# A two-layer streaming encoder step on one core: norms summed and spread by one wide product, norm weights loaded with x, sample softmax transposed a step later, and prompt scores as three float32r products

## The chip, the cores and the metric

The kernel runs on one core of one Trainium2 chip. The metric is the device time in microseconds of one execution; the time before is the median of three runs. The profile is of one further execution. PE is TensorE (matmuls), PEld its weight loads, DVE is VectorE, ACT is ScalarE, POOL is GpSimd, SP is SyncE, which issues most DMAs. The kernel writes matmuls of two kinds: float32, which the trace shows as two records each, and float32r, which it shows as one.

## The reference

An encoder of two layers reads a prompt of 256 frames and a sample of 32 frames with a cache of 128. The width is 1024, heads have 64 features.

```
layer 0: x += concat(8 chunked softmax heads with a relative bias,
                     8 stick-breaking heads) @ w_out_ab
layer 1: x += 16 forgetting heads @ w_out_c      # softmax(q k / 8 + cum_q - cum_k)
both:    x += 4-head cross-attention(rmsnorm(x)) into 256 memory rows
         x += (silu(h @ w_gate) * (h @ w_up)) @ w_down,  h = rmsnorm(x)
rmsnorm(x) = x * rsqrt(mean(x * x) + 1e-6) * g       # 7 norms of x, 1 of the memory's rows a layer
```

Outputs are the final norm of both streams and the new keys, values, log-forget values and memory keys and values. Everything is float32.

## The kernel before

Activations are held with features on partitions: `x` is eight tiles of 128 features by 288 tokens (256 prompt tokens and 32 of the sample). Every weight matrix comes in units of 128 x 1024 (512 KB). `unit` loads one by a DMA of SP into `st`, ACT casts it to float32r (`hi`, L156), and DVE subtracts (`lo`, L157). The normed input is split likewise into `hh` and `hl`, and `mm3` (L183) makes each block of a projection from three float32r products (hh hi, hl hi, hh lo), so that about float32 precision results. A unit of eight blocks is 24 products of 288 columns into one accumulator `pj`, of which there are four. The down projection of the feed-forward part is `dn`, the output projections are `op`, the memory's values `mv`.

The norm is split off: `Next.block` multiplies x by the norm's weight `gain` only and projects that; the token's scale `rstd` is applied when an accumulator is evacuated (L668, L760, L762, L795, L802). `Norm.add` squares each block on ACT (`sq`) and adds it up on POOL, the last on DVE (`ssq`). `columns` (L266) sums over the partitions by three float32 products against `mean1`, of two columns each (`nrm`), and `newton` (L275) makes the inverse root by eleven DVE operations on 128 x 6 numbers; `rows` (L287) spreads it over all partitions by three more products (`nr`), and ACT copies the result into `rstd` (L331). Until then, evacuations are held back in `waiting`. `begin` starts two units with six of eight blocks before the last blocks of x are there, and calls `columns` behind the first unit.

Attention is written as generators, which `tick` advances by one step after each unit, so that attention work stands between projections. `attend_prompt` (L414) handles a pair of heads, which lie in the two halves of the partitions: it transposes v (`vt`), multiplies q and k of each head in float32 (`sc`, 64 rows, 128 and 256 columns), and runs `softmax` (L394) on DVE and ACT into `e`; two steps later it transposes the weights (`tp`) and one step after that multiplies by v (`po`). `attend_sample` (L451) does the same for four heads of the sample (`ss`, `es`, `ts`, `os`, then `ot`). In layer 1 the bias `bc` of a pair is made on POOL (L1001 to L1004) from a row `ck`, which comes by a DMA. The gate's own product is `gp`, and its logits are folded by `gt` after rstd.

The order on each engine is set by the scheduler of the framework when the program is built; each engine then runs its own instructions strictly in that order. `not_before` adds an order by hand.

Of the kernel before, what the change touches and what calls it, by code (L numbers as in the profile page):

```python
# [15 lines left out]
P = 128  # L16
# [10 lines left out]
def encoder_step(ctx: ExitStack, tc: tile.TileContext, a):  # L27
# [21 lines left out]
    def tok(s, dt=F32):  # L49
        return tk.tile([P, NT], dt, tag="t", name=name(s))  # L50
# [19 lines left out]

    gain = cst.tile([P, 9 * KT], F32, name="gain")
    xh = [big.tile([P, 2 * NT], F32, tag=f"x{i}", name=f"x{i}") for i in range(4)]
    x = [xh[k // 2][:, (k % 2) * NT:(k % 2) * NT + NT] for k in range(KT)]

# [5 lines left out]

    def x_part(i, eng=DMA):
        eng.dma_start(xh[i], a["xT"][:, 2 * i * NT:2 * (i + 1) * NT])

    first_part(0, 0, 384)
    x_part(0)
    x_part(1, S)
    x_part(3, S)
    DMA.dma_start(gain, a["gains"])
    first_part(0, 384, 1024)
    first_part(1, 0, 1024)  # L90
    x_part(2)
    first_part(2, 0, 1024)


    mean1 = cst.tile([P, 2], F32, name="mean1")
    G.memset(mean1, 1.0 / 1024.0)
    identb = cst.tile([P, P], BF16, name="identb")
    make_identity(nc, identb)


    line = cst.tile([8, 384], F32, name="line")
    lined = dr.tile([8, 384], F32, name="lined")
# [37 lines left out]
    def more_constants():  # L140
        V.tensor_scalar(ident, warm[:, 0:P], 1.0 / 32.0, None, op0=ALU.mult)
        by_head = ident.rearrange("p (j i q) -> p j i q", j=2, i=2)
        V.tensor_tensor(fold, by_head[:, :, 0], by_head[:, :, 1], ALU.add)
        V.tensor_tensor(fold4, fold[:, 0, 0:16], fold[:, 1, 0:16], ALU.add)
        V.tensor_copy(ntrir, ntri)

# [52 lines left out]
    def begin(srcs, cur):  # L199


        out = []
        for src in srcs:
            w, p = unit(src), acc("pj")
            for k in range(BEGIN):
                mm3(p[:, :NT], w, k, cur.h, k, k == 0, False)
            out.append((w, p))
            if len(out) == 1:
                cur.y = cur.norm.columns()
        return out  # L210
# [30 lines left out]
    class Norm:  # L241
# [7 lines left out]
        def add(self, xb, eng=None):  # L249
            q = tok("sq")  # L250
            S.activation(q[:, :self.n], xb[:, :self.n], AF.Square)  # L251
            self.parts += 1
            eng = eng or (V if self.parts == KT else G)
            i = int(self.parts == KT and self.hurry)
            if self.acc[i] is None:
                self.acc[i] = q
            else:
                s = tok("ssq")
                eng.tensor_tensor(s[:, :self.n], self.acc[i][:, :self.n], q[:, :self.n], ALU.add)  # L259
                self.acc[i] = s  # L260

        def sum(self, p, part, begin):
            for i, t in enumerate(self.tiles):
                mm(p[:, 2 * i:2 * i + 2], part[:, t:t + 128], mean1, begin and i == 0, False)

        def columns(self, between=None):  # L266
            p = att("nrm")
            self.sum(p, self.acc[0], True)
            if between:
                between()  # L270
            if self.acc[1] is not None:
                self.sum(p, self.acc[1], False)
            return self.newton(p)

        def newton(self, p):  # L275
            c = len(self.tiles)
            v, y, t = small("ms"), small("y"), small("nt")
            v, y, t = v[:, :2 * c], y[:, :2 * c], t[:, :2 * c]
            V.tensor_scalar(v, p[:, :2 * c], EPS, None, op0=ALU.add)
            V.tensor_scalar(y.bitcast(I32), v.bitcast(I32), -0.5, 1597463007.0, op0=ALU.mult, op1=ALU.add)  # L280
            for _ in range(3):
                V.tensor_tensor(t, y, y, ALU.mult)
                V.scalar_tensor_tensor(t, t, -0.5, v, op0=ALU.mult, op1=ALU.mult)
                self.last = V.scalar_tensor_tensor(y, t, 1.5, y, op0=ALU.add, op1=ALU.mult)
            return y

        def rows(self, y):  # L287

            p = att("nr")
            for i, t in enumerate(self.tiles):  # L290
                a0 = 256 if i == 2 else t
                mm(p[:, a0:t + 128], y[:, 2 * i:2 * i + 1].to_broadcast([P, P]), ident[:, a0 - t:P], i == 0, True)
            return p[:, :self.n]

# [10 lines left out]
    class Next:  # L305


        def __init__(self, gi):
            self.gi, self.norm, self.h, self.waiting = gi, Norm(hurry=gi == 8), ([], []), []
            self.y = None  # L310

# [12 lines left out]

        def scale(self):

            if self.gi == 0:
                yield 1
            p = self.norm.rows(self.y)
            self.r = big.tile([P, NT], F32, tag="rstd", bufs=2, name=name("rstd"))  # L330
            r = S.copy(self.r, p)  # L331
            done = [f() for f in self.waiting]
            self.waiting = None
            if self.gi == 0:
                behind.append(self.norm.last.ins)
                yield 1
                behind.extend([r.ins, done[-1].ins])

# [75 lines left out]
    def attend_prompt(q, k, v, vns, j, bias, oh, ol, at=None, falling=False):  # L414

        q0, q1 = (q[:, 160:288], q[:, 32:160]) if falling else (q[:, 0:128], q[:, 128:256])
        vn = vns[j] = v_natural(v)
        e = []
        for hd in range(2):
            r = slice(64 * hd, 64 * hd + 64)  # L420
            s = att("sc")
            mm(s[:, 0:128], q0[r], k[r, 0:128])
            mm(s[:, 128:384], q1[r], k[r, 0:256])
            e.append(work("e"))
            softmax(s, QT, bias[hd], e[hd], at)
# [25 lines left out]
    def attend_sample(qs, ks, two, vns, ck, cv, bias, o, falling=False):  # L451
# [7 lines left out]
        e = work("es")  # L459
        softmax(s, [(0, 160)], bias, e)  # L460
        yield 1
        t = att("ts")
# [115 lines left out]
    def mem_scales():  # L578
        y = memn.columns()
        V.tensor_copy(memcol, y.rearrange("p (t two) -> p t two", two=2)[:, :, 0])  # L580
        S.copy(memrow, memn.rows(y))

    class Memory:
# [28 lines left out]
        def step(self):  # L612
# [10 lines left out]
            else:  # L623
# [15 lines left out]
                if half == 1:  # L639
                    for t in range(2):  # L640
                        v = tok("mv")
                        V.tensor_scalar(v[:, 0:NP], self.p[:, 256 * t:256 * t + 256], memcol[:, t:t + 1], None, op0=ALU.mult)
                        store(a["mv"][l, t, :, hd * 256:hd * 256 + 256], v[:, 0:NP])
                        self.v[t, hd] = split(v[:, 0:NP], tok("vh", F32R)[:, 0:NP], tok("vl", F32R)[:, 0:NP])


    def cross(layer, cur, memory, nxt):
        o = ([tok("oh", F32R) for _ in range(KT)], [tok("ol", F32R) for _ in range(KT)])
        q, qs = [], []
        begun = begin([a["w_xq"][layer, f] for f in range(2)], cur)  # L650
        active.append(cur.scale())

# [101 lines left out]
    def ffn(layer, cur, nxt, ahead):  # L754
        h = ([], [])
        active.append(cur.scale())

# [64 lines left out]
    def mix_ab(cur, nxt, memory, w0):  # L822
# [6 lines left out]
        def side_by_side():  # L829
            p = [att("pj"), acc("pj"), acc("pj")]  # L830
            with tc.issue_after(warmed.ins):
                for k in range(KT):
                    for u in range(3):
                        b = 3 * k + u
                        i = mm3(p[u][:, :NT], w0[b // 8], b % 8, cur.h, k, k == 0, k == KT - 1)
                        if k in (0, 5, 7) and u == 2:
                            began.append(i.ins)
            cur.y = cur.norm.columns()
            tick()
            return p  # L840

        def proj(j):
# [7 lines left out]
            if j < 4:  # L850
                biases[j] = [rel_prompt(2 * j + i) for i in range(2)]
            vs[j] = evac_kv(cur, next(p), a["kv0"][kv + 4])

# [20 lines left out]

        active.append(cur.scale())
        pairs(proj, attend, sample, memory, (0, 0, 0, 0, 2, 2, 2, 8))
# [99 lines left out]
    def mix_c(cur, nxt, memory, w0):  # L976
# [3 lines left out]
        begun = begin([w[0], w[8]], cur)  # L980
        active.append(cur.scale())
        p = att("gp")
# [55 lines left out]
    cur.norm.add(x[KT - 1], V)  # L1038
    more_constants()
    memories = [Memory(0), Memory(1)]  # L1040
# [46 lines left out]
def _pack(inputs):  # L1087
# [17 lines left out]
    def vals(c):  # L1105
# [3 lines left out]
    gains = np.stack([g["g_mix"][0], g["g_mix"][1], g["g_xattn"][0], g["g_xattn"][1], g["g_mem"][0], g["g_mem"][1],  # L1109
                      g["g_ffn"][0], g["g_ffn"][1], g["g_final"]])  # L1110
    w_ab = units(g["w_in_ab"][0])
# [3 lines left out]
    out = {  # L1115
        "xT": feats(x), "memT": feats(g["mem_prompt"][0]),
        "gains": gains.reshape(9, 8, 128).transpose(2, 0, 1).reshape(128, 72),
        "w_ab": w_ab, "w_first": w_ab[[0, 4, 8]].reshape(3, 128, 8, 128).transpose(1, 2, 0, 3).reshape(128, 3, 1024).transpose(1, 0, 2), "w_oab": units(g["w_out_ab"][0]),
# [41 lines left out]
```

## Time and profile before

| | |
|---|---|
| median of 3 runs | 957.79 us (957.63 to 958.33) |
| profiled execution | 958.14 us, span 956.4 us |
| first projection product, first norm's sum | 7.26 us, 18.88 us |
| softmax heads of layer 0, of layer 1 | up to about 75 us, 515 to 635 us |
| cross-attention | about 191 to 247 us and 657 to 713 us |
| feed-forward | 270 to 480 us and 737 to 945 us |
| last norm and output | from 945.5 us |

A row of a group shows line, engine, operation, what it writes and reads, shape and count, then the busy time in us and the mean ns of one, then the engine's idle time ahead of it and what ended it. A row of the timeline starts with the start and the length in us. A row of the chain of waits has start, length, and what was waited for or done. Matmuls overlap: the length of one record is longer than its distance to the next, and the distance is what counts.

### The profile page before, as it was taken

What the parts mean: (1) busy time and instruction counts of PE and PEld (TensorE: products, weight loads), DVE (VectorE), ACT (ScalarE), POOL (GpSimd) and SP (SyncE); (2) the same over time, 40 slices, a digit from 0 to 9 for tenths busy, and PEclk for the clock granted to TensorE, in tenths of its full rate; (3) what the DMA queues carried; (4) which work ended last, traced back from release to release, by engine and by line L of the source; (5) the groups of instructions that cost most, each with busy time, mean ns of one, the idle gap of its engine ahead of it and who ended that gap; (6) DMA issues with size and microseconds to landing.
All of it is one profiled execution on the core that took longest, in us unless ns stands there. A gap on an engine that the chain in (4) does not pass through costs nothing.

```text
span 956.4 us, 19036 instructions
## 1 busy us (share of the span) xinstructions
PE 943.6 (99%) x7476; PEld 915.0 (96%) x7476; DVE 587.3 (61%) x1137; ACT 483.8 (51%) x860; POOL 237.2 (25%) x358
## 2 busy tenths in 40 slices
PE   8999999999999999999999999999999999999997
PEld 8988999999999999999999989999999999999996
DVE  6876556676665555854565666668657655555442
ACT  5666777545554444444455554555445544444431
POOL 4331123400222222410124352432012222222010
PEclk9999999999999999999999999999999999999999
DMA  7665445543444444554466455545425544454431
GB/s 266 208 213 195 155 169 183 183 160 116 142 157 160 171 161 170 176 199 170 160 205 206 168 191 177 184 152 190 139 95 176 168 163 170 162 175 159 174 111 50
DMA packets 49258, 160.97 MB, mean 168 GB/s; under 512 B 7304, under 2 KB 8136, under 8 KB 49168
## 3 DMA queue, kind: packets, MB, share of 16 engines
q1 hardware_dynamic: 44976, 149.12, 45.5%
q0 software_dynamic: 3904, 10.04, 3.0%
q8 instruction: 59, 0.97, 0.4%
q10 hardware_dynamic: 288, 0.59, 0.2%
q14 instruction: 31, 0.25, 0.1%
HBM read 149.58 MB, written 10.15 MB: 167 GB/s over the span
## 4 chain that ended last, share of the span: by engine, by line
PE 84%; issue 11%; DVE 2%; DMA 1%; POOL 1%; ACT 0%; DVEq 0%; SPq 0%; POOLq 0%; ACTq 0%
PE pj L68 49%; PE dn L68 15%; PE op L68 9%; PE mv L68 4%; PE po L68 1%; PE sc L68 1%; PE zb L68 1%; DMA st<-w_ab 1%; DMA gain<-gains 1%; PE nrm L68 0%; PE os L68 0%; POOL ssq L259 0%; PE zs L68 0%; PE nr L68 0%; DVE e L410 0%
## 5 line engine op out<-in xcount | busy, mean ns | idle before, releaser
L156 ACT CAST hi<-st 128x1024 fp32r<-128x1024 f32 x257 | 269.3, 1049 | 312.2 <-issue 140.8
L68 PE MATMUL pj<-hh,hi 128*128 128x288 f32 (+1 forms) x1344 | 400.2, 298 | 1.1 <-ACT hh L299 1.1
L68 PE MATMUL pj<-hl,hi 128*128 128x288 f32 (+1 forms) x1344 | 395.2, 294 | 0.0
L68 PE MATMUL pj<-hh,lo 128*128 128x288 f32 (+1 forms) x1344 | 395.2, 294 | 0.0
L157 DVE TENSOR_TENSOR lo<-st,hi 128x1024 fp32r<-128x1024 f32 x257 | 318.6, 1240 | 94.1 <-PE dn L68 43.0
L68 PEld LDWEIGHTS pj<-hh,hi 128*128 128x128 f32 x1344 | 253.3, 188 | 7.6 <-issue 4.8
L68 PEld LDWEIGHTS pj<-hl,hi 128*128 128x128 f32 x1344 | 253.5, 189 | 0.3 <-DVE hl L302 0.3
L68 PEld LDWEIGHTS pj<-hh,lo 128*128 128x128 f32 x1344 | 253.2, 188 | 0.0
L68 PE MATMUL dn<-fh,hi 128*128 128x288 f32 x400 | 108.8, 295 | 0.0
L68 PE MATMUL dn<-fh,lo 128*128 128x288 f32 x352 | 103.7, 295 | 0.0
L68 PE MATMUL dn<-fl,hi 128*128 128x288 f32 x304 | 89.6, 295 | 0.0
L68 PE MATMUL op<-oh,hi 128*128 128x288 f32 x256 | 76.1, 298 | 0.0
L68 PE MATMUL op<-ol,hi 128*128 128x288 f32 x256 | 75.5, 295 | 0.0
L68 PE MATMUL op<-oh,lo 128*128 128x288 f32 x256 | 75.4, 295 | 0.0
L68 PEld LDWEIGHTS dn<-fh,hi 128*128 128x128 f32 x400 | 72.4, 188 | 0.0
L68 PEld LDWEIGHTS dn<-fh,lo 128*128 128x128 f32 x352 | 66.1, 188 | 0.0
L259 POOL TENSOR_TENSOR ssq<-ssq,sq 128x288 f32<-128x288 f32 (+1 forms) x35 | 34.9, 996 | 120.3 <-ACT sq L251 78.4
L767 POOL TENSOR_TENSOR fl<-us,fh 128x288 fp32r<-128x288 f32 x38 | 33.8, 889 | 120.1 <-ACT fh L766 120.1
L762 DVE TENSOR_TENSOR us<-pj,rstd 128x288 f32<-128x288 f32 x44 | 20.1, 457 | 62.6 <-PE pj L68 62.6
L763 POOL TENSOR_TENSOR gs<-gs,sg 128x288 f32<-128x288 f32 x44 | 39.3, 893 | 72.8 <-ACT sg L761 72.8
L68 PEld LDWEIGHTS dn<-fl,hi 128*128 128x128 f32 x304 | 57.0, 188 | 0.0
L68 PEld LDWEIGHTS op<-oh,hi 128*128 128x128 f32 x256 | 48.0, 188 | 0.7 <-issue 0.4
(268 smaller groups left out, 1255.0 us busy)
## 6 DMA issues: line engine op xcount, KB each, us to landing
st<-w_gate SPq DMA_DIRECT2D x44, 512.0 KB
st<-w_up SPq DMA_DIRECT2D x44, 512.0 KB, 3.2
st<-w_down SPq DMA_DIRECT2D x44, 512.0 KB, 3.2
st<-w_c SPq DMA_DIRECT2D x24, 512.0 KB, 4.0
st<-w_ab SPq DMA_DIRECT2D x21, 512.0 KB, 6.1
st<-w_xk SPq DMA_DIRECT2D x16, 512.0 KB, 4.4
st<-w_xv SPq DMA_DIRECT2D x16, 512.0 KB, 3.8
st<-w_xq SPq DMA_DIRECT2D x16, 512.0 KB, 3.3
```

The costliest lines, as they stand in the source:

```text
L68: return T.matmul(out, lhsT, rhs, start=start, stop=stop, skip_group_check=True)
L156: a = S.copy(hi, st[:, c0:c1])
L157: b = V.tensor_tensor(lo, st[:, c0:c1], hi.bitcast(F32), ALU.subtract)
L259: eng.tensor_tensor(s[:, :self.n], self.acc[i][:, :self.n], q[:, :self.n], ALU.add)
L762: V.tensor_tensor(us, pu[:, :NT], cur.r, ALU.mult)
L763: G.tensor_tensor(gs, gs, sg, ALU.mult)
L767: G.tensor_tensor(lo, us, hi.bitcast(F32), ALU.subtract)
```

## The change

It has six parts.

1. **Wide norms.** For the five norms in the middle, `wide` splits the last sum into float32r halves `qh` and `ql` (the names that the splits of queries have, too), and two products with a 128 x 128 matrix `meanr` of 1/1024 give the mean over features on all partitions at once. `rsqrt` then makes the inverse root by eight DVE operations, here on 128 x 288 numbers, and writes `rstd`. The small epsilon is added to the second sum, which thereby is always DVE's. The first norm, the memory's and the last keep `columns`, with the shorter `rsqrt` on 128 x 6.
2. **Its place.** `begin` calls it inside the second unit, behind 27 products, where `columns` stood behind 20; there is no row product any more.
3. **Loading.** `gain` lies in front of x's first block in one tile, and both come by one DMA, the first on ACT's queue; the other x and weight parts are reordered. The identity is made on ACT, other constants later.
4. **Sample softmax.** `attend_sample` lets one more step pass between softmax and transposes.
5. **Memory values.** The last head's `vl` is DVE's, not POOL's.
6. **Scores.** `attend_prompt` splits q (ACT and POOL) and k (ACT and DVE) into float32r halves, and each score block is three products; heads alternate, so that products on the two halves of the partitions follow each other.

```diff
-            cur.y = cur.norm.columns()          # begin: behind the first unit
+                if out and k == 2:
+                    cur.scale()
...
+        def rsqrt(self, v, y, t, out):
+            V.tensor_scalar(y.bitcast(I32), v.bitcast(I32), -0.5, 1595932665.0, op0=ALU.mult, op1=ALU.add)
+            V.tensor_tensor(t, y, y, ALU.mult)
+            V.scalar_tensor_tensor(t, t, -0.375 * 0.703952253, v, op0=ALU.mult, op1=ALU.mult)
+            V.scalar_tensor_tensor(y, t, 0.375 * 0.703952253 * 2.38924456, y, op0=ALU.add, op1=ALU.mult)
+            V.tensor_tensor(t, y, y, ALU.mult)
+            V.scalar_tensor_tensor(t, t, 64.0 / 9.0, v, op0=ALU.mult, op1=ALU.mult)
+            V.scalar_tensor_tensor(t, t, -10.0 / 3.0, t, op0=ALU.add, op1=ALU.mult)
+            self.last = V.scalar_tensor_tensor(out, t, 5.0, y, op0=ALU.add, op1=ALU.mult)
+        def wide(self):
+            hi, lo = split(self.acc[0], tok("qh", F32R), tok("ql", F32R), V)
+            p = att("nrm")[:, :self.n]
+            mm(p, meanr, hi, True, False)
+            mm(p, meanr, lo, False, True)
+            r = big.tile([P, NT], F32, tag="rstd", bufs=2, name=name("rstd"))
+            self.rsqrt(p, tok("y"), tok("nt"), r)
...
     def attend_prompt(q, k, v, vns, j, bias, oh, ol, at=None, falling=False):
-        q0, q1 = (q[:, 160:288], q[:, 32:160]) if falling else (q[:, 0:128], q[:, 128:256])
+        c0 = 32 if falling else 0
+        qq = split(q[:, c0:c0 + 256], tok("qh", F32R)[:, 0:256], tok("ql", F32R)[:, 0:256])
+        kk = split(k[:, 0:256], tok("kh", F32R)[:, 0:256], tok("kl", F32R)[:, 0:256], V)
         vn = vns[j] = v_natural(v)
-        for hd in range(2):
-            r = slice(64 * hd, 64 * hd + 64)
-            s = att("sc")
-            mm(s[:, 0:128], q0[r], k[r, 0:128])
-            mm(s[:, 128:384], q1[r], k[r, 0:256])
+        s, e = [att("sc") for _ in range(2)], []
+        for qt, (c0, c1) in enumerate(QT):
+            b = slice(128 * qt, 128 * qt + 128) if not falling else slice(128 - 128 * qt, 256 - 128 * qt)
+            for i, (qi, ki) in enumerate(((0, 0), (0, 1), (1, 0))):
+                for hd in range(2):
+                    r = slice(64 * hd, 64 * hd + 64)
+                    mm(s[hd][:, c0:c1], qq[qi][r, b], kk[ki][r, 0:c1 - c0], i == 0, i == 2)
...
         softmax(s, [(0, 160)], bias, e)          # attend_sample
         yield 1
+        yield 1
...
+    S.dma_start(xh[0][:, 0:G0 + NT], a["xT"][:, 0:G0 + NT])      # gain and x's first block
+    S.dma_start(xh[1], a["xT"][:, G0 + 2 * NT:G0 + 4 * NT])
     first_part(0, 0, 384)
-    x_part(0)
-    x_part(1, S)
-    x_part(3, S)
-    DMA.dma_start(gain, a["gains"])
...
-                        self.v[t, hd] = split(v[:, 0:NP], ...)
+                        self.v[t, hd] = split(v[:, 0:NP], ..., V if hd == 3 else G)
```

Three places of the built order. On TensorE, the norm ahead of the first cross-attention: before, its sum stands in the second unit's products and its rows 22 products later.

```order
L68 MATMUL pj_2688<-hh_2370,hi_2684 128x288
L68 MATMUL pj_2688<-hl_2371,hi_2684 128x288
L68 MATMUL nrm_2664<-mean_95,ssq_2604 128x2 x3
L68 MATMUL pj_2688<-hh_2370,lo_2685 128x288
...
L68 MATMUL pj_2645<-hh_2598,lo_2642 128x288
L68 MATMUL nr_2713<-ident,y_2669 128x128 x2
L68 MATMUL nr_2713<-ident,y_2669 128x32
L68 MATMUL pj_2688<-hh_2558,hi_2684 128x288
```

And after:

```order
L68 MATMUL pj_2729<-hl_2458,hi_2725 128x288
L68 MATMUL pj_2729<-hh_2457,lo_2726 128x288
L68 MATMUL nrm_2743<-qh_2739,meanr 128x288
L68 MATMUL nrm_2743<-ql_2740,meanr 128x288
L68 MATMUL pj_2729<-hh_2497,hi_2725 128x288
L68 MATMUL pj_2729<-hl_2498,hi_2725 128x288
```

Six float32 products at two places became two float32r products at one, seven products later.

On POOL, pair 3 of layer 1 (`kv` is the store of a key or value, `bc` the pair's bias). Before:

```order
L231 DMA kv<-kv_6994 128x288
L1001 TENSOR_TENSOR bc_7040<-cumcol,ck_7038 128x128
L1002 TENSOR_TENSOR bc_7040<-cumcol,ck_7038 128x256
L1004 AFFINE_SELECT bc_7040<-bc_7040 128x128 x2
L1001 TENSOR_TENSOR bc_7049<-cumcol,ck_7038 128x128
L1002 TENSOR_TENSOR bc_7049<-cumcol,ck_7038 128x256
L1004 AFFINE_SELECT bc_7049<-bc_7049 128x128 x2
L231 DMA kv<-kv_7035 128x288
```

And after:

```order
L237 DMA kv<-kv_7083 128x288
L1026 TENSOR_TENSOR bc_7129<-cumcol,ck_7127 128x128
L1027 TENSOR_TENSOR bc_7129<-cumcol,ck_7127 128x256
L1029 AFFINE_SELECT bc_7129<-bc_7129 128x128 x2
L1026 TENSOR_TENSOR bc_7138<-cumcol,ck_7127 128x128
L1027 TENSOR_TENSOR bc_7138<-cumcol,ck_7127 128x256
L1029 AFFINE_SELECT bc_7138<-bc_7138 128x128 x2
L389 TENSOR_TENSOR ql_7179<-q_7038,qh_7178 128x256
L237 DMA kv<-kv_7124 128x288
```

The query's split stands behind the whole bias; in pairs 1, 2, 4 and 6 it stands ahead of it.

On TensorE, pair 2 of layer 0 and the first sample. Before, the sample's products stand directly behind the previous pair's, and the scores directly behind the transposed values:

```order
L68 MATMUL po_787<-pt_737,vn_581 64x128
L68 MATMUL os_794<-ca_610,pts_742 32x64 x4
L68 MATMUL os_794<-vn_462,pts_742 32x64 x2
L68 MATMUL os_794<-vn_581,pts_742 32x64 x2
L386 MATMUL vt_806<-ident,kv_745 128x128
L387 MATMUL vt_806<-ident,kv_745 128x128
L388 MATMUL vt_806<-ident,kv_745 32x128
L68 MATMUL sc_813<-kv_677,q_614 128x128
L68 MATMUL sc_813<-kv_677,q_614 128x256
```

And after (ten products of the next unit stand where the row of dots is):

```order
L68 MATMUL po_812<-pt_768,vn_600 64x128
L487 MATMUL ts_819<-ident,es_698 128x128
L488 MATMUL ts_819<-ident,es_698 32x128
L404 MATMUL vt_833<-ident,kv_770 128x128
L405 MATMUL vt_833<-ident,kv_770 128x128
L406 MATMUL vt_833<-ident,kv_770 32x128
...
L68 MATMUL sc_840<-kh_829,qh_825 128x128
L68 MATMUL sc_841<-kh_829,qh_825 128x128
L68 MATMUL sc_840<-kl_830,qh_825 128x128
```

The scores moved ten products down, and the sample's products (`os`) moved behind the rest of that unit, where they stand between full-size products.

More of the change, by code (lines that the diff above doesn't have):

```diff
@@ L256, in add @@
                 self.acc[i] = q
-            else:
[L258 to L264, printed above, removed]
-        def columns(self, between=None):
[L267 to L284, printed above, removed]
-            return y
@@ L287, in rows @@
[L287 to L293, printed above, removed]
+                return
+            s = tok("ssq")
+            b, c = self.acc[i][:, :self.n], q[:, :self.n]
+            if self.parts == 2:
+                V.scalar_tensor_tensor(s[:, :self.n], b, EPS * KT, c, op0=ALU.add, op1=ALU.add)
+            else:
+                eng.tensor_tensor(s[:, :self.n], b, c, ALU.add)
@@ L580, in mem_scales @@
         V.tensor_copy(memcol, y.rearrange("p (t two) -> p t two", two=2)[:, :, 0])
-        S.copy(memrow, memn.rows(y))
+        p = att("nr")
+        for i in range(2):
+            mm(p[:, 128 * i:128 * i + 128], y[:, 2 * i:2 * i + 1].to_broadcast([P, P]), ident, i == 0, True)
+        S.copy(memrow, p[:, :NP])
     class Memory:
@@ L837, in side_by_side @@
                             began.append(i.ins)
-            cur.y = cur.norm.columns()
+            start(cur.first_scale())
             tick()
```

82 lines of the change are left out of this document (50 added, 32 removed).

## The prediction

> **What bounds the kernel now.** I read the page first, then the table of stretches, the chain of waits, the waits of TensorE's weight loads, and the timeline at the places that the diff touches.
>
> ```profile
> PE 943.6 (99%) x7476; PEld 915.0 (96%) x7476; DVE 587.3 (61%) x1137; ACT 483.8 (51%) x860; POOL 237.2 (25%) x358
> 7.30:25.00 17.70, 17.70 (x121) 17.43 (x122) 15.34 (x41) 11.75 (x26) 5.97 (x16) 1.00 0.78 275
> 50.00:75.00 25.00, 24.25 (x195) 22.01 (x194) 21.68 (x63) 15.79 (x41) 8.33 (x14) 1.00 0.63 212
> 515.00:635.00 120.00, 119.65 (x1044) 109.83 (x1043) 78.08 (x218) 64.06 (x160) 50.59 (x99) 1.00 0.54 186
> ```
>
> The columns of the stretches are length, then busy time of PE, PEld, DVE, ACT and POOL, clock, DMA share, GB/s. TensorE has work in 943.6 of 956.4 us, and in both softmax stages (50:75 and 515:635) it stands still for under 1 us. So time is gained by fewer or shorter TensorE instructions, and at the two ends, where TensorE does not work yet or no more. DVE is loaded too, to 87% in 50:75 and 87% at the start: what is added there can become a TensorE wait.
>
> The sum is made against the profiled execution, 958.14 us (span 956.43 and 1.7 around it); the median of the runs shown, 957.79, is 0.35 lower, and I carry that difference over at the end.
>
> **The wide norms** replace, for five of the norms, three float32 sums, three float32 row products and an ACT copy by two float32r products of 288 columns.
>
> ```profile
> 268.07 2.65 PE pj L68 x20
> 270.71 0.66 PE nrm L68 x6
> 271.38 3.02 PE pj L68 x22
> 274.40 0.59 PE nr L68 x6
> 270.04 0.45 DVE L259 TENSOR_TENSOR ssq<-ssq,sq 128x288 f32<-128x288 f32 x1
> 275.73 0.46 DVE L760 TENSOR_TENSOR gs<-pj,rstd 128x288 f32<-128x288 f32 x1
> 409.39 70.03 PE dn L68 x528
> ```
>
> A 288-column product takes 70.03/528 = 0.133 us, so each norm goes from 0.66 + 0.59 = 1.25 us to 0.27 on TensorE: 0.98 less, times five **-4.9**. Both new products need the last sum (ends 270.49) split first, an ACT cast and a DVE subtraction of about 0.45 each: ready at 271.4. They stand 27 products behind the start at 268.07, so at 271.65: 0.25 us of cover. A slip on ACT or DVE is paid in full; between 0 and 0.5 a norm, I take **+0.4** in all. Then rstd: eight DVE operations of 0.46 (as the one at 275.73), each waiting for the one before, with two weight casts of 1.2 between them, some 6.2 us in place of 11 x 0.2 and the row product. The evacuations wait for it, but four accumulators of 24 products (3.2 us each) lie ahead, 36 of those 96 products already issued at the start; the first that must be free again is needed 13 us after 268.07, and rstd comes after about 10.4. Free of cost, except in layer 1, where the gate's fold product now stands about where rstd and two more DVE operations end: **+0.2**. What is late next is the q split of the first cross head, with about 1 us left.
>
> **Scores.** Per pair of heads four float32 products (eight records, 768 columns) become twelve float32r products, which alternate between the heads' two row halves.
>
> ```profile
> 515.28 0.27 PE L387 MATMUL vt<-ident,kv 128*128 128x128 f32 x1
> 515.39 0.27 PE L388 MATMUL vt<-ident,kv 128*32 128x128 f32 x1
> 515.59 0.93 PE L68 MATMUL sc<-kv,q 64*128 64x128 f32 x8
> 516.46 0.39 PE L68 MATMUL pj<-hh,hi 128*128 128x256 f32 x1
> 515.59 0.53 PEld L68 LDWEIGHTS sc<-kv,q 64*128 64x128 f32 x8 [0.21 <-PE vt L387]
> 515.59:515.80 0.21, 0.21 (x2) 0.21 (x4) 0.00 (x0) 1.00 1.07 372
> 516.14:516.45 0.31, 0.31 (x4) 0.00 (x0) 0.00 (x0) 1.00 0.70 283
> 97.90 0.28 PE L68 MATMUL pj<-hh,lo 128*128 128x256 f32 x1
> 98.02 0.28 PE L68 MATMUL pj<-hh,hi 128*128 128x256 f32 x1
> ```
>
> Eight weight loads of 128 columns fit in 0.53 us and eight products in 0.87 (515.59 to 516.46), and two start in each short stretch: the two halves of the array work side by side. One head alone takes 0.11 + 0.11 for 128 columns and twice 0.22 for 256, with 0.1 on either side to change between full rows and halves. The new form, if the halves still run together, takes 3 x 0.11 (a 128-column product with weights of its own, 515.28 to 515.39) and 3 x 0.12 (256 columns, 97.90 to 98.02): 0.69 in place of 0.66. So the products gain nothing: **+0.1** for twelve pairs, where the row for 128 columns is the doubt. Ends: if 128 columns cost half of 256, 0.06, it is 12 x -0.12 = -1.4; if the halves do not run together, 12 x 0.69 = +8.3.
> The Trainium skill, TensorE: Matmul & The Clock Gate, "Back-to-back issue gap", gives about 81 ns a product for a stream of loads and products of 128 columns; the row here says 110. By the Trainium skill's figure the scores would save about 1.0 us (an estimate), by the row nothing.
>
> What the splits add: per pair two ACT casts (0.4 each), a DVE subtraction (0.42) and one on POOL, and TensorE now waits for these, not for the evacuation alone.
>
> ```profile
> L371 POOL TENSOR_TENSOR vl<-mv,vh x16: 734/749/1610, 155.3 to 710.1; 128x256 fp32r<-128x256 f32 x16
> 552.31 0.53 POOL L1004 TENSOR_SCALAR_AFFINE_SELECT bc<-bc 128x128 f32<-128x128 f32 x2
> 554.37 0.86 PE sc L68 x8
> 50.12 0.86 PE sc L68 x4
> 55.25 1.40 DVE e L410 x4
> ```
>
> In layer 1, for pairs 3, 5 and 7, POOL's queue has the split behind the pair's bias, which itself waits for a DMA. Of pair 3 the bias ends at 552.84; a POOL subtraction of the same shape takes 0.75 (up to 1.61), which makes 553.6, and the scores come at 554.3: 0.7 of cover, gone if POOL is slow once. In layer 0, pairs 2 and 3 have the key's split on ACT behind the copy of the transposed values, so that it comes some 2.4 us after the transposes, and the ten products put between cover 1.7. And there the scores come ten products later while the transposes of the weights stay: these had 48 products of cover, now 38 (5.0 us), where the softmax took from 50.1 to 56.6. I take **+2.0** for all waits at the scores; ends 0 and +6 (half a microsecond at each of the twelve).
>
> **Smaller parts.**
>
> ```profile
> PEld xo L68 <- POOL vl L371: 1.5, 2, 0.7
> PEld ts L463 <- DVE es L410: 0.7, 1, 0.7
> L463 PE MATMUL ts<-ident,es 128*128 128x128 f32 x6 | 1.7, 286 | 0.8 <-DVE es L410 0.8
> PEld os L68 <- issue: 1.4, 8, 0.2
> 947.87 0.18 DVE ms L279
> 949.87 0.18 DVE y L284
> ```
>
> The split of the last memory values moves from POOL to DVE: TensorE's two waits of 0.7 go, **-1.2** (ends 0 and -1.5). The sample softmax one step later takes away the waits of its transposes: **-1.0** (0 to -1.5). The price: six sample products (os) stand by themselves between full-size products, no longer behind the pair's own, and such a group pays its change of tiles, 0.2 at eight entries: **+1.0** (0 to +1.5). The last norm has eight small DVE operations for eleven (947.87 to 949.87 is ten steps of 0.2), at the very end: **-0.6**.
>
> **The start.** The norm weights travel with the first block of x, first on ACT's queue.
>
> ```profile
> 2.57 3.60 PE L134 MATMUL warm<-identb 128*128 128x128 bf16 x32 [2.57 <-POOL identb masks.py:199]
> 1.74 4.85 DMA gain<-gains
> 6.67 0.54 ACT hh L299
> 7.26 11.78 PE pj L68 x72
> 7.26:11.30 4.04, 4.04 (x15) 3.77 (x16) 1.00 1.02 414
> 11.30:19.04 7.74, 7.74 (x62) 7.74 (x60) 1.00 0.81 258
> ```
>
> Now ACT waits until 6.67 for the small transfer that was issued third, while the warm-up products end at 6.17. With weights and first block on one early transfer TensorE should go on at about 6.0: -1.2. The 15 products up to 11.30 take 0.27 each, those behind them 0.125: they run at half pace, although the clock column says 1.00, which costs 15 x 0.14 = 2.1 us. Without the gap the full pace may come earlier. DVE, busy 15.3 of 17.7 us here, and the arrival of the weights cap the gain, though 0.9 us of constants leave DVE's start. I take **-2.0**; ends 0 (the first weights or x arrive no earlier) and -3.3.
>
> **Sum:** -4.9 + 0.4 + 0.2 + 0.1 + 2.0 - 1.2 - 1.0 + 1.0 - 0.6 - 2.0 = -6.0: 952.1 for a profiled execution, **951.8** as a median.
>
> **Rivals.** (1) Slower: the float32r half-array products run one after the other. Nothing in the trace is a float32r product on 64 rows; all that overlap are float32. Place: the twelve score groups, 0.86 us each now, 1.55 then. Price +8.2: 960.0. It decides once a group takes over 0.86 + 6.0/12 = 1.36 us. Against it: the overlap shows for the weight loads as well as the products, so it belongs to the rows, not to the number type. 0.10.
> (2) The splits come late everywhere: scores wait 0.5 us in all twelve places, and the norms 0.5 each. For it: POOL's 1.61 and DVE's 87%. 951.8 + 4.0 + 2.0 = 957.8 at the end, 956.3 in the middle. 0.16.
> (3) Full pace comes early at the start and no score waits: -1.3 - 2.0 = 948.5. The Trainium skill, TensorE: Matmul & The Clock Gate, Part 1, says that the clock is released after about 3.4 us of unbroken work, in windows that run freely. The trace agrees so far as work without a gap from 7.26 came to full pace at 11.3, and 3.6 us of warm-up with a gap behind it did not. 0.14.
>
> **How the numbers follow.** 0.60 for my forecast, with 949.5 to 954.5 as its own range. The range 947.5 to 957.2 takes in rival 3 and most of rival 2, and leaves rival 1 out. No change means within 0.2%, 955.9 to 959.7, about what such a measurement can tell: most of the upper half of rival 2 (0.08) and a little of rival 1 (0.03) fall there. Slower is the rest of rival 1 and a little for what I have not seen, 0.09; faster 0.80.
>
> **What would show it.** Right: each norm as two products in about 0.27 us with no idle time ahead; score groups of some 0.7 to 0.9 us with twelve records; no idle time of xo and ts; the first projection near 6.0 us and full pace before 10. Wrong: score groups of 1.4 us; idle time ahead of sc that ends with ql or kl; xs or gt waiting for rstd; idle time ahead of tp in 50:75.

## The result and the profile after

The changed kernel took 951.72 us as a median of five executions (951.46 to 955.12), the kernel before 958.08 in the same job: a ratio of 0.994, interval 0.9923 to 0.9958. So it is faster by some 6 us. Six more executions on another chip gave 953.68 (950.38 to 955.31). All eleven together fall in two groups, seven between 950.4 and 952.8 and four between 954.6 and 955.3; the profiled execution, 955.12, is one of the upper group. What most likely makes the groups is the main finding below: a stall of TensorE, and the half pace that follows it in some executions.

The page's first line and four stretches of the changed kernel, in the columns of before:

```profile
PE 940.9 (99%) x7474; PEld 913.8 (96%) x7474; DVE 604.5 (63%) x1141; ACT 492.2 (52%) x885; POOL 237.3 (25%) x359
```

```profile
7.30:25.00 17.70, 17.70 (x133) 17.23 (x132) 15.43 (x35) 12.49 (x28) 7.53 (x19) 1.00 0.89 303
50.00:75.00 25.00, 23.12 (x182) 21.23 (x183) 19.89 (x59) 14.22 (x38) 8.60 (x14) 0.86 0.56 184
515.00:635.00 120.00, 120.00 (x1073) 111.36 (x1072) 83.80 (x223) 68.76 (x172) 55.31 (x104) 1.00 0.54 183
...
66.00:69.00 3.00, 3.00 (x17) 2.77 (x18) 2.41 (x13) 1.28 (x7) 0.34 (x1) 0.50 0.15 57
```

In the first stretch TensorE starts 133 products where it started 121: the earlier start. In layer 1's softmax (515 to 635) its last idle 0.35 us are gone. In layer 0's (50 to 75) it now stands still for 1.88 us, and the clock column, 1.00 before, falls to 0.86, in the three microseconds from 66 to 0.50. That is new.

Here is TensorE's timeline at the feed-forward's norm, and at the first scores of layer 1:

```profile
272.84 0.30 PE L68 MATMUL pj<-hh,lo 128*128 128x288 f32 x1
272.97 0.29 PE L68 MATMUL nrm<-qh,meanr 128*128 128x288 f32 x1
273.10 0.30 PE L68 MATMUL nrm<-ql,meanr 128*128 128x288 f32 x1
273.24 0.30 PE L68 MATMUL pj<-hh,hi 128*128 128x288 f32 x1
...
515.60 0.33 PE L68 MATMUL sc<-kh,qh 64*128 64x128 f32 x2
515.77 0.27 PE L68 MATMUL sc<-kl,qh 64*128 64x128 f32 x2
...
516.28 0.28 PE L68 MATMUL sc<-kh,ql 64*128 64x256 f32 x2
```

The norm's two products take 0.27 us and wait for nothing. The scores' records come in pairs (x2), so both heads run at once; the next full product starts at 516.49, 0.89 after the first, where it was 0.87.

Now the place at 63 us, pair 3 of layer 0, first on ACT, then on TensorE:

```profile
62.78 1.05 ACT L162 CAST hi<-st 128x1024 fp32r<-128x1024 f32 x1 [1.46 <-DMA st<-w_ab]
63.74 0.36 ACT L399 CAST oh<-po 128x256 fp32r<-128x256 f32 x1
...
64.73 0.40 ACT L388 CAST kh<-kv 128x256 fp32r<-128x256 f32 x1
...
63.35 0.29 PE L68 MATMUL pj<-hh,hi 128*128 128x288 f32 x1
65.18 0.33 PE L68 MATMUL sc<-kh,qh 64*128 64x128 f32 x2 [1.53 <-ACT kh L388]
```

ACT waits 1.46 us for a weight DMA, casts that unit, and only then comes to `oh`, the copies of the transposed values, `qh` and `kh`, for which TensorE waits. From 63.35 to 65.18 it starts one product instead of some fourteen. What follows runs at half pace: the clock column reads 0.50 from 65.72 to 72.55 and 1.00 on either side.

Three rows of the waits of TensorE's weight loads show what else is new:

```profile
PEld gc L68 <- DVE lf L958: 1.5, 1, 1.5
PEld sc L68 <- DVE kl L389: 1.3, 3, 0.5
...
PEld xt L710 <- DVE xq L694: 0.8, 2, 0.4
```

The waits of `xo` for `vl` and of `ts` for `es` are gone; the gate's cumulative products (`gc`) wait 1.5 us for the gate's last DVE operation, three score groups for `kl`, and the first cross head waits for its queries (`xq`).

To set sizes beside the prediction, I added up in each trace the distance from a product's start to the next one's, tile by tile (a wait ahead of the next product is in it, so the wait ahead of a group stands in the row of the tile before it, mostly `pj`). The last column is an experiment told below, the changed kernel with a single ACT instruction moved.

| us | before | changed | one cast moved |
|---|---|---|---|
| up to the first projection product | 7.26 | 5.91 | 5.92 |
| nrm, nr | 9.45 | 4.58 | 4.54 |
| sc | 11.54 | 12.90 | 12.39 |
| xo | 12.98 | 11.39 | 11.39 |
| tp, ts | 9.72 | 8.52 | 8.52 |
| os | 3.95 | 3.95 | 3.95 |
| xss, xt (first cross head) | 7.59 | 8.95 | 8.95 |
| pj | 538.09 | 542.05 | 538.41 |
| dn | 139.97 | 139.54 | 139.54 |
| behind the last product | 7.18 | 6.48 | 6.49 |
| span | 956.43 | 953.42 | 948.81 |

### The profile page after: what moved, and what is told of

The parts are those of the page before. It is cut to its first block, busy times and chain, and to the rows that moved or that the text cites. A ratio compares the mean times of both kernels' runs of the same rounds, so it can differ in the third digit from the quotient of the medians.

```text
span 953.4 us, 19089 instructions
## 1 busy us (share of the span) xinstructions
PE 940.9 (99%) x7474; PEld 913.8 (96%) x7474; DVE 604.5 (63%) x1141; ACT 492.2 (52%) x885; POOL 237.3 (25%) x359
## 4 chain that ended last, share of the span: by engine, by line
PE 95%; DVE 1%; DMA 1%; ACT 1%; issue 0%; DVEq 0%; POOL 0%; POOLq 0%; ACTq 0%; SPq 0%
PE pj L68 54%; PE dn L68 15%; PE op L68 11%; PE mv L68 5%; DMA st<-w_ab 1%; PE xs L68 1%; PE xo L68 1%; PE po L68 1%; PE sc L68 1%; PE zb L68 1%; PE xss L68 1%; DVE lo L163 0%; PE xt L710 0%; PE zs L68 0%; PE warm L140 0%; PE os L68 0%
```

## The experiments

**The changed kernel again.** No edit.

> The changed kernel as it is, for a second profile. In the first one TensorE stood still for 1.5 us at 63.6, waiting for the key's cast of pair 3, and its clock column then said 0.50 to 0.64 until 72.5, which cost some 4 us; that execution took 955.1 us, the other four 951.5 to 952.1. Theory A: that was an accident of one late transfer. Then the new profiled execution takes 951 to 952.5 us, the clock column is 1.00 from 60 to 80, and the wait at pair 3 is under 1 us. Theory B: the wait belongs to the kernel, and only the profiled execution shows it: 954.5 to 955.5 again, with the half clock at the same place.

Measured: 953.68 (950.38 to 955.31); the profiled execution 954.57, with the same stall, 2.57 us long this time, and half pace behind it:

```profile
66.00:69.00 3.00, 2.68 (x17) 2.32 (x18) 2.94 (x12) 1.06 (x5) 1.07 (x2) 0.67 0.00 1
```

Theory A is out: the stall belongs to the kernel, and theory B has the place right. B does not say why seven executions were 3 us shorter. A stall without the half pace behind it would make that difference; three profiles of other kernels below have just that. For the short executions themselves it isn't shown, since none of them was profiled. Their mean granted clock is on record and points that way without parting the groups: 0.997 to 1.000 in the seven, 0.995 to 0.998 in the four.

**Scores in float32 again.**

```diff
-        qq = split(q[:, c0:c0 + 256], ...)
-        kk = split(k[:, 0:256], ..., V)
...
+            mm(s[:, 0:128], q0[r], k[r, 0:128])
+            mm(s[:, 128:384], q1[r], k[r, 0:256])
```

> The changed kernel with the scores of the prompt's softmax heads as four float32 products a pair again, without the splits of q and k. Theory A, from the first trace after: the group of products takes 0.02 to 0.03 us more than before (0.3 in all), and the splits cost three waits in layer 0 (0.4, 0.7 less the 0.45 that stood there before, and pair 3's), so without them the time falls by 1 to 2 us, to 949.7 to 950.7. Theory B, the forecast's sum: part 6 cost 2.1, of which a part in layer 1: 949.6. Theory C: the float32r products are the cheaper ones, and the time rises by about 1 us to 952.7.

Measured: 951.94 (951.09 to 953.91), 1.7 below the changed kernel of the same job, the step that A forecast, though the intervals of the two overlap (0.9924 to 0.9948 and 0.9930 to 0.9963 of the time before). But the trace shows another reason than mine: no stall at 63, one at 75, and half pace behind that (0.89 from 80 to 90).

```profile
74.85 1.05 ACT L162 CAST hi<-st 128x1024 fp32r<-128x1024 f32 x1 [2.29 <-DMA st<-w_xk]
...
76.07 0.37 ACT L408 COPY vn<-vt 128x256 f32<-128x256 f32 x1
...
76.64 0.70 PE L68 MATMUL zb<-q,kv 64*128 64x256 f32 x2 [1.07 <-ACT vn L409]
```

Again a weight cast that waits for its DMA, with an evacuation behind it. So this run can't price part 6, and it says that such a stall does not need the splits.

**The old order of loads.**

```diff
-    S.dma_start(xh[0][:, 0:G0 + NT], ...)       # gain and x's first block, on ACT's queue
...
+    first_part(0, 0, 384)
+    DMA.dma_start(xh[0][:, G0:G0 + 2 * NT], ...)
...
+    DMA.dma_start(gain, a["xT"][:, 0:G0])
```

> The changed kernel with the loads in the order of before: the first weights, then x's first two blocks, the norm weights by a transfer of their own behind these, the other blocks of x on ACT's queue. Theory A: the early norm weights let TensorE start 1.35 us sooner and reach full pace sooner, 2.0 to 2.3 us in all: 953.7 to 954.0. Theory B: what is gained at the start is lost again by 28 us, where the weights' subtractions on DVE had only 0.7 us of slack: 951.7.

Measured: 955.62 (951.95 to 956.88), 1.9 over the changed kernel of the same job. TensorE starts at 7.36, where it was 7.26 before, and its 121st projection product, at 28 us, comes 0.5 later than before, where the changed kernel's comes 1.7 earlier. So the loading is worth 2.2 us at that point, theory A, and keeps them past the stretch with little slack; the times alone overlap too much to say so. The stall at pair 3 is here too, 2.6 us long, although TensorE started late: it does not need the early start.

**The narrow norms again.**

```diff
-                if out and k == 2:
-                    cur.scale()
+            if len(out) == 1:
+                cur.y = cur.norm.columns()
...                                          # row products and copy as before
```

> The changed kernel with the five middle norms as before (three float32 sums behind the first unit, the root on 128 x 6 numbers, three float32 row products, a copy on ACT), with the shorter root. Theory A: the wide norms save 0.98 us on TensorE each, and give back the 1.3 us that TensorE waits in layer 1 for the gate: 4.9 - 1.3 = 3.6, so 955.3. Theory B: the gate's wait is there with either norm (it comes from the order of the steps), and the full 4.9 come back: 956.6. Theory C: wide norms cost waits for their splits that the trace hides in other rows: under 954.5.

Measured: 958.17 (955.95 to 960.11), 4.5 over the changed kernel of the same job, between A's 3.6 and B's 4.9, so the time can't choose. The trace can: `nrm` and `nr` are back at 9.52, the gate's wait is gone, and `xss` and `xt` are back at 7.59. The wide root thus causes both new waits, 1.3 us for the gate and 1.4 for the two first cross heads together, against theory B. A wait of 0.9 us at the first scores of layer 1 has come instead (they wait for POOL's query split), and the stall at 63 is there, 1.66 us long and without half pace behind it.

**Splits earlier; and with it the gate a step later; and the gate alone.** In the first the splits of q and k follow the key's evacuation directly:

```diff
+                if j > 0:
+                    split_qk(j, qs[j], ks[j], True)     # layer 0, in proj, behind ks[j]
...
+            split_qk(j, qs[j], ks[j])                   # layer 1, behind ks[j]
...
-        for _ in range(4):                              # gate, in the second and third
+        for _ in range(5):
             yield 1
         c = att("gc")
```

> The changed kernel with the splits of q and k written right behind the key's evacuation, one projection before the scores, for all pairs but the very first. In both traces after, the key's cast of pair 3 stands on ACT behind a weight cast that waits for its DMA until 62.8 to 63.6, and TensorE stands still for 1.5 to 2.4 us there; then the clock column shows half pace for some 7 us. Theory A: the stall comes from the order on ACT alone. The scores of pairs 1, 2 and 3 wait no more, the half pace goes with the stall, and the time falls by 2 to 4 us to 948 to 950, with a spread under 1.5 us. Theory B: the weights' DMA is the limit of this stage, TensorE having come to it 2.5 us early; then the stall moves to the next product that needs a weight or the copy of the transposed values (vn is behind the same cast), between 62 and 76, and the time stays at 951 to 955.

> As the one before, and the gate's cumulative products (gc) one step later. Theory A: both waits go, 947 to 949. Theory B: what was in the way of the splits moves, and only the gate's 1.3 us come back: 950 to 954.

> The changed kernel with the gate's cumulative products (gc) one step, 21 products, later. In the traces after TensorE waits 1.26 us for the gate's last DVE operation there, at 497 us; with narrow norms it does not. Theory A: the wait goes and nothing needs the cumulative sums before the first pair's bias, some 10 us on: 1.3 us less. Theory B: the bias of the first pair is then late, the first scores' softmax too, and what goes at 497 comes back by 530 as a wait at the transposes: no change.

Measured: 954.43 (952.80 to 957.87), 954.15 (952.88 to 956.03) and 953.12 (951.12 to 953.91). The first:

```profile
75.75 1.05 ACT L162 CAST hi<-st 128x1024 fp32r<-128x1024 f32 x1 [2.21 <-DMA st<-w_xk]
...
76.97 0.38 ACT L408 COPY vn<-vt 128x256 f32<-128x256 f32 x1
...
77.54 0.70 PE L68 MATMUL zb<-q,kv 64*128 64x256 f32 x2 [1.46 <-ACT vn L409]
```

```profile
80.00:85.00 5.00, 5.00 (x47) 4.68 (x46) 2.85 (x12) 4.00 (x6) 0.54 (x1) 0.81 0.04 15
```

The scores of pair 3 wait no more, but the stall moved to 75 and the half pace with it, as theory B had it. In the third, the gate's wait went and came back:

```profile
512.73 1.22 POOL L389 TENSOR_TENSOR ql<-q,qh 128x256 fp32r<-128x256 f32 x1
...
514.00 0.33 PE L68 MATMUL sc<-kh,ql 64*128 64x128 f32 x2 [1.57 <-POOL ql L389]
```

The first pair's bias is made later now, and POOL has it and a store's issue ahead of the query split, for which TensorE waits 1.57 us. No change, theory B, though the place is the scores and not the transposes. In the second, where the splits are early as well, that wait does not come, and the gate's own is 0.7 instead of 1.4. Its stall at 76 (1.2 us) and the half pace behind it remain, and its 954.15 is out of theory A's range and just above theory B's.

**The heads one after the other.** All six products of head 0, then those of head 1.

```diff
-            for i, (qi, ki) in enumerate(...):
-                for hd in range(2):
+        for hd in range(2):
+            for qt, (c0, c1) in enumerate(QT):
```

> The changed kernel with the twelve score products of a pair written head after head, six and six, in place of alternating. Theory A: the two halves of the rows take their products from the one order each by itself, as in the profile before, where the records of both heads start 13 ns apart although head 0's four passes are written first: the group stays at 0.88 us. Theory B, from rival 1: only neighbouring products overlap, so the group takes 0.88 + 0.5 or more, 1.4 us, and the kernel 6 us longer.

Measured: 955.85 in the one execution, groups of 1.17 us, between A's 0.88 and B's 1.4. TensorE's timeline:

```profile
518.39 0.32 PE L68 MATMUL sc<-kh,qh 64*128 64x128 f32 x1
518.55 0.27 PE L68 MATMUL sc<-kl,qh 64*128 64x128 f32 x1
518.66 0.27 PE L68 MATMUL sc<-kh,ql 64*128 64x128 f32 x1
518.67 0.43 PE L68 MATMUL sc<-kh,qh 64*128 64x128 f32 x2
```

Head 1's first product, written seventh, starts 0.28 us after head 0's first, when three of head 0 have started. So the halves run side by side for float32r too, and the written order costs only this delay of the second head: 0.28 a group, 3.4 for twelve. Neither theory holds as it stands. Rival 1's price of 0.69 a group was too high even for this order.

**All evacuations ahead of the casts.** In layer 0 from pair 2 on, every later weight cast is ordered behind the attention's ACT work; the second kernel adds the two changes in layer 1.

```diff
+        if hold and first_layer[0] and evacs:
+            not_before(a, evacs[-1])
```

> The changed kernel, but in layer 0 from pair 2 on a weight unit's cast on ACT stands behind the attention's evacuations (vn, kh, oh) that are written ahead of it. The scheduler sets the order of the rest again. In the traces so far the weights cast at 63.6 and 75.8 are not used until 16 to 20 us later, yet ACT waits for their DMAs with the evacuations behind them. Theory A: ACT's order alone made the stalls of TensorE at 63 and 75 and the half pace after them; both go, and the time falls by 3 to 4 us against the changed kernel, to 949 to 950, with all executions within 1.5 us. Theory B: the weights' loop of load, cast and subtraction is the limit; the casts, now later, make the weights late, TensorE waits for hi or lo after 70 us, and the time is 952 or more.

> As the one before, and in layer 1 the gate's cumulative products one step later and the splits of q and k right behind the key's evacuation. Theory A: in the trace of the kernel with the gate's step later alone, its 1.26 us came back as 1.57 us at the first pair's scores, which waited for POOL's query split behind the bias; with the split early there is no such wait, and 0.7 to 1.3 us more are gained than by the ACT order: 948 to 949. Theory B: POOL and ACT are in the way elsewhere in layer 1, and the time is as in the kernel before, 949 to 950.

Measured: 970.13 (969.66 to 970.51) and 970.33 (970.12 to 971.25), 1.3% slower than before. TensorE's waits in the first:

```profile
PEld pj L68 <- ACT hi L162: 4.1, 6, 1.1
...
PEld pj L68 <- DVE lo L163: 2.4, 6, 0.7
```

In the changed kernel neither is among the twenty longest. Pushed back as a rule, the weights came late: these two rows make 6.5 us, where the span is 15 longer than the changed kernel's (968.3 against 953.4). The rest is spread over attention rows (the scheduler set the orders anew) and was not followed up, and pair 3's scores still wait 1.2 us for `kh`. Theory B for the first, by far; for the second kernel neither theory's 948 to 950.

**One cast moved.** The same hint for a single instruction, the fifth unit's cast behind pair 3's `kh`. On ACT one row moves by five places; on TensorE and DVE no row moves.

```diff
+        if casts:
+            casts.append(a)
+            if len(casts) == 6:
+                not_before(a, casts[0])      # casts[0]: kh of pair 3
```

> The changed kernel with one instruction moved and no other: on ACT, the weight cast that waits for its DMA until 63.6 stands behind the five casts and copies of pair 3 (oh, vn, qh, vn, kh), not ahead of them. Its weights are first used 16 us later. The kernel that moved all such casts was 1.3% slower, since its weights came with 0.1 us to spare or late. Theory A: the stall at 63 is this one place, and the half pace behind it comes from the stall. Both go: TensorE's idle time there is under 0.5 us, the clock column stays 1.00, and the time is 949 to 951 in every execution. Theory B: the delayed cast shifts the wait to the next evacuation behind a waiting cast, as at 75 in the kernel with early splits; the half pace comes there, and the time stays at 951 to 955.

> As the one before, and in layer 1 the gate's cumulative products one step later and the splits of q and k right behind the key's evacuation. Theory A: 0.5 to 1.3 us less than the one before, since the gate's wait of 1.4 is 0.7 in the two kernels that had both of these, and no scores wait in layer 1: 948 to 950. Theory B: no change against it.

Measured: 950.35 (950.01 to 950.74), ratio to before 0.9918 (0.9904 to 0.9931); with the two changes in layer 1, 950.08 (949.64 to 950.49), 0.9915 (0.9901 to 0.9928). ACT and the stretches of the first:

```profile
62.84 0.40 ACT L392 CAST kh<-kv 128x256 fp32r<-128x256 f32 x1
63.15 1.04 ACT L162 CAST hi<-st 128x1024 fp32r<-128x1024 f32 x1
```

```profile
63.00:66.00 3.00, 2.68 (x24) 2.24 (x24) 2.96 (x13) 2.20 (x6) 1.66 (x2) 1.00 0.73 239
66.00:69.00 3.00, 3.00 (x36) 2.80 (x35) 2.81 (x13) 2.84 (x10) 0.61 (x1) 1.00 0.21 55
```

The key's cast is done 1.9 us sooner and the weight cast 0.36 later, with 17.6 us left until its first product. TensorE starts 36 products from 66 to 69 where it started 17, at full clock, and all executions lie within 0.75 us. Theory A for the first. For the second the time shows 0.3 us, inside the intervals; the spans, 948.81 and 948.01, differ by 0.8, of which 0.7 is the gate's shorter wait:

```profile
PEld gc L68 <- DVE lf L972: 0.8, 1, 0.8
```

Both medians lie below both kernels'. The intervals of the ratios overlap with the changed kernel's (0.9923 to 0.9958), but of its eleven executions ten were slower than all nine of these two kernels.

## Why the prediction was right

The forecast was 951.8 us, its own range 949.5 to 954.5, and both medians, 951.72 and 953.68, lie in it. That the first is within 0.1 us is luck: the terms were off by up to 1.4 us, both ways, and the largest wait had a cause that the prediction did not name. One of its signs of being wrong did appear, idle time ahead of `sc` that ends with `kl`. By its steps, from the table:

- **Norms, -4.9:** 9.45 to 4.58, -4.9. The waits for the split, +0.4: none; the distance ahead of `nrm` is 0.13 in all five. That the root is free of cost failed: the first cross head's queries come late, 0.7 us in each layer (+1.4 in `xss` and `xt`), the place that the step named as late next, with about 1 us to spare by its count.
- **Gate, +0.2:** +1.3. The step sized the first consumer, the fold product `gt`, which does not wait, and not the last: `gc` now stands 55 products behind `gt`, where it stood 92 behind, and the chain of DVE and ACT between them does not end in time for that.
- **Score products, +0.1:** 0.02 to 0.03 a group, 0.3. Rival 1 is out.
- **Waits at the scores, +2.0:** the sum came about right for executions without half pace, the mechanism did not. The step put half a microsecond at many places; pair 0 waits 0.4 for `kl`, pair 3 0.5, pair 2 is cheaper than before by 0.4 (its group ran over 2.04 us there), and no pair of layer 1 waits. Nearly all of the cost is the one stall at 63, 1.7 us, and in some executions up to 2.9 more by the half pace (4.6 is the whole gap between the spans 953.42 and 948.81, and 1.7 of it the stall). The prediction named POOL's queue behind the pair's bias, and for ACT only the copy of the transposed values ahead of the key's cast; that a weight cast waiting for its DMA stands ahead of them on ACT was in the trace before as well, behind scores that had started at 63.93:

```profile
64.77 1.05 ACT L156 CAST hi<-st 128x1024 fp32r<-128x1024 f32 x1 [3.39 <-DMA st<-w_ab]
```

- **vl, -1.2:** -1.6. **Sample softmax, -1.0:** -1.2 (`tp` and `ts`). **The isolated `os` groups, +1.0:** about +0.5. The row itself is 3.95 both times, since a group pays its change of tiles next to other attention work too. But the step into a group stands in the row before it: from a full-size product it is 0.20 to 0.23 us, where the next full-size product would follow after 0.13, for six groups.
- **Last norm, -0.6:** -0.7.
- **The start, -2.0:** -2.3 by the fourteenth product. The first comes at 5.91 and full pace at 7.7:

```profile
4.76 0.54 ACT L312 ACTIVATE hh<-x 128x288 fp32r<-128x288 f32 x1 [1.51 <-DMA x<-xT]
...
5.91 0.59 PE L68 MATMUL pj<-hh,hi 128*128 128x288 f32 x1
...
7.50 0.39 PE L68 MATMUL pj<-hh,hi 128*128 128x288 f32 x1
7.73 0.29 PE L68 MATMUL pj<-hl,hi 128*128 128x288 f32 x1
```

Seven products run at half pace instead of fifteen; that half of rival 3 held, its other half (no score waits) did not. That the gap behind the warm-up makes the difference fits all profiles: three to eight products run at half pace in the twelve without the gap, 15 and 12 in the two with it (before, and the old order of loads, where ten at full pace come first). The trace's clock records begin only at 7.70, and at 11.27 before; the 1.00 that the column shows ahead of these has no record behind it.

So +1.4, +1.1 and +0.2 were missed on the side of cost, and -0.5, -0.4, -0.4, -0.3 and -0.2 on the other, with -0.4 from `dn`, which nobody touched: its 1056 products take 0.4 ns less each. A few tenths stay unassigned. Without the stall the same change gives 7.8 us (950.35 against 958.12).

## What to carry to other kernels

An engine that works strictly in its order, and casts prefetched data as well as evacuating results, must not have a cast whose data is still on its way ahead of an evacuation that the bottleneck waits for: here one such row cost 1.7 to 4.6 us, and moving it by five places cost nothing, since its data was not needed for another 17 us. Move the one row that the trace names; the same hint given to all of them made the kernel 1.3% slower. When a change makes the bottleneck engine run ahead, look for the transfers that do not come earlier by as much. In the run with float32 scores TensorE came to the last transpose of the values at 74.44 us, 3.5 earlier than before (77.92), but the weight cast ahead of their copy on ACT ran only 1.5 earlier (74.85, before 76.38). Before, that cast waited for TensorE; in that run it waited for its transfer, and the stall at 75 followed. The rows of before, then that run's transpose:

```profile
77.92 0.27 PE L388 MATMUL vt<-ident,kv 128*32 128x128 f32 x1
76.38 1.05 ACT L156 CAST hi<-st 128x1024 fp32r<-128x1024 f32 x1 [2.61 <-PE pj L68]
...
74.44 0.27 PE L406 MATMUL vt<-ident,kv 128*32 128x128 f32 x1
```

## What was not expected of the hardware

A stall of TensorE may cost more than itself. Eleven profiles here have one of 1.2 to 2.6 us between 63 and 78, with a second of 0.2 to 0.5 close behind in most. In eight of them the clock then falls to 0.50 for 3.41 us, or for 6.83 in two; in three (the narrow norms, the heads one after the other, and the second kernel with all evacuations ahead) it stays at 1.00 behind 1.66, 1.38 and 1.36. The single wait of 1.2 to 1.4 at the gate is never followed by it, in eight profiles.

Where a fall can come is fixed: in every profile all changes of the clock lie whole multiples of 3.41 us apart (in the changed kernel at 7.70, 65.72, 72.55 and 949.77), so the clock changes only at the borders of windows of this length, which run on whatever TensorE does, and each of the eight falls comes at the first border behind the stall. The position of the windows matters. The two kernels with all evacuations ahead do the same work there, with TensorE busy for 2.01 of the 3.41 us from 66.10, but the borders are at 69.51 in the first and at 67.04 and 70.45 in the second. These are the rows behind it, the first kernel's, then the second's (where a stall of 1.6 us at 165, which both have, is followed by a fall at 166.03, and not in the first):

```profile
69.52:72.92 3.40, 3.40 (x17) 3.40 (x16) 3.27 (x12) 2.08 (x10) 0.84 (x1) 0.50 0.47 166
69.52:72.92 3.40, 3.40 (x40) 3.21 (x39) 3.40 (x13) 2.07 (x9) 0.84 (x1) 1.00 0.49 167
```

It is not all that matters. With the gate's step later and with the heads apart the windows lie alike (borders at 66.05 and 65.99), each with the stall inside and TensorE busy for 1.87 of 3.40 us, and the clock falls in one alone:

```profile
66.06:69.46 3.40, 3.40 (x22) 3.12 (x24) 2.14 (x13) 2.28 (x9) 0.00 (x0) 0.50 0.01 2
65.99:69.40 3.41, 3.41 (x41) 3.08 (x41) 3.06 (x15) 1.99 (x9) 0.51 (x1) 1.00 0.18 70
```

What else decides stays open. The Trainium skill, TensorE: Matmul & The Clock Gate, "Why this matters for your kernels", warns of idle gaps above about 3 us; here 1.2 was enough in two profiles, and the measurement decides.

Products of different row halves start out of written order, so "strictly in that order" does not hold for TensorE: in the run with the heads apart, head 1's 128-column product starts at 518.67, 0.1 ahead of head 0's first 256-column one (the second record of that row), which is written before it. For that run the written order is all that is shown, but the kernel before has the same: its built order, of which one pair is shown above, has both products of a head next to each other, and both heads' records start 13 ns apart. The Trainium skill, TensorE: Matmul & The Clock Gate, "The mechanism", has matmuls start and end in the program's order; this trace differs.

The same 288-column product has a slightly different pitch in different programs: 132.0 ns in the second `dn` stage of the changed kernel, in both its profiles, 132.5 before, 132.8 with the narrow norms. Over a stage of 528 such products that is 0.4 us, as much as several terms of the sum.
